# mLSTM gate preparation: two TensorE transposes replaced by VectorE-and-DMA turns, started one group earlier, with a head's masks added beside its keys

## The chip, the cores and the metric

The kernel runs on one core of a Trainium2 chip. The metric is device time in microseconds, from the first instruction to the last plus what lies around them. The core has a matrix engine (TensorE, "PE" in the profile, with its weight loads as "PEld"), VectorE (DVE), ScalarE (ACT), GpSimd (POOL) and SyncE (SP). SP computes nothing here; it issues most of the DMA transfers. Each engine takes its instructions strictly in the order of its own list and waits on semaphores for the others.

## The reference

One encoder block on 512 tokens of width 1024, all in float32:

```python
h = rms_norm(x, mix_norm_g[l])
proj = h @ w_in[l]      # mLSTM q,k,v,o,gates | attention q,k,v | memory q | merge gates
y_ml = mlstm_branch(...)             # 4 heads of 128, two directions
y_na = neighbourhood_attention(...)  # 8 heads on an 8 x 64 grid
y_xa = memory_cross_attention(...)   # 4 heads, 256 memory tokens
merged = g_ml * (y_ml @ w_br_ml[l]) + g_na * (y_na @ w_br_na[l]) + g_xa * (y_xa @ w_br_xa[l])
x = x + merged @ w_out[l]
x = x + conv_glu_ffn(rms_norm(x, ffn_norm_g[l]), ...)
return rms_norm(x, final_norm_g)
```

The change concerns the gates of the mLSTM. For each token, head and direction there is an input gate and a forget gate. The branch needs the running sum of the logarithm of the forget gate along the tokens of a chunk, and a running maximum that keeps the exponentials in range:

```python
log_f = jax.nn.log_sigmoid(f_pre)
a = jnp.cumsum(log_f, axis=-1)
D = a[..., :, None] - a[..., None, :] + log_i[..., None, :]
D = jnp.where(causal, D, -jnp.inf)
m_j = jnp.maximum(a + m_prev[..., None], jnp.max(D, axis=-1))
P = jnp.exp(D - m_j[..., None]) * qk
h = num / jnp.maximum(jnp.abs(den), jnp.exp(-m_j))[..., None]
```

The kernel computes the same with chunks of 128 tokens.

## The kernel before

**Matmuls.** Nearly every product is made in three passes (`mm3`, L334): both operands are split into a rounded high part and a low remainder, and high x high, high x low and low x high are added in PSUM. Activations are kept as high and low tiles (`XH`/`XL`, `NH`/`NL`). Weights come from DRAM in blocks of 1024 columns and more, three raw buffers ahead (`emit_raw`, L189, loads on SP). Each half of a block becomes a high piece by a ScalarE copy (L301) and a low piece by a VectorE subtraction (L302); there are four buffers for such pairs, so TensorE's progress frees them.

**The order of the stages.** First come the mLSTM queries and keys (feature-major), then three "token-major" groups (`TMW`, L598 to L620), in which the tokens lie on the partitions of the result: group 0 gives the gates `Gt` and half of the values, group 1 the other half and some attention values, group 2 the rest of the attention values. Inside a group the loop goes over weight blocks `h`, then over the four token tiles `t`, then over `k`. Then come four projections `xaq` (memory queries), four `o` (output gates), four `memk` and the four steps of `memv` (memory keys and values), four `naq` and four `nak` (attention queries and keys), and then three branches, each with merge gates and a projection. In a projection, 8 x 3 matmuls run on 512 tokens (256 for `memk`). The output projection and the feed-forward part follow.

**Steps between matmuls.** The mLSTM, the memory attention and the neighbourhood attention are Python generators (`ml_all`, `xa_all`, `na_all`), one behind the other in the list `gens`. `step(n)` (L1124) adds n to a quota and resumes the first generator once for each whole unit; the projections call it with 0.65 in the middle and 0.65 at the end (`mid`, `RB`), the memory blocks with 0.65 for each block, the merge gates with half a unit twice. Each `yield` ends a step. So the generators' small matmuls are placed in TensorE's list between the large ones. The first branch calls `drain` (L1204) before it reads the mLSTM result. The build's scheduler keeps this program order as a priority, but may place an instruction of VectorE, ScalarE, GpSimd or SP earlier on its engine where its inputs are ready.

**The gate preparation** (`ml_prep`, L637 to L730) has four steps:

1. the logarithm of the forget gate as 32 columns `lf`, by some twenty small VectorE operations;
2. `lfc` (tokens on partitions; log-forget at columns 0 and 32, input gate at 64 and 96) is turned into rows by four TensorE transposes with the identity (L670). ScalarE copies 36 of the rows (L672), and four scans on VectorE (L676, L677, L685, L686) make the running maximum `mr` and the running sum `cu`; a copy of `cu` goes to rows 64 to 100 of `mr`;
3. `rr = cu - mr`, written to DRAM as `rd`, and the chunk ends as a small diagonal tile `dg`;
4. the rows of head 0 are loaded broadcast to all partitions (`load_R`), head 0's turned keys are loaded (`turn_in`), four more TensorE transposes (L712) bring `mr` back to tokens on partitions, a product of ones with `dg` (L714) spreads the chunk ends, and the exponentials `em`, `bi`, `ex` follow.

**A turn** is what the kernel already uses for keys, heads and attention weights: `turn_out` (L166) transposes the 32 x 32 blocks of a 128 x 512 tile on VectorE (L169) and stores the result with four DMAs (L172) to a DRAM tile `td`; `turn_in` (L176) loads that tile (L178) with tokens and features exchanged.

**A head** is then `begin` (products of keys and queries L761, scaling of turned keys L764/L765), `middle` (states L801, L806, first diagonal tile L774/L778), `rest` (second diagonal tile), `last` (queries L788/L790, and the loads of the next head's rows and keys), and four `values_J` steps (L817 to L828). The rows `R` plus a causal mask are the masked rows `rm`; today `load_R` adds the masks (L742) as soon as the rows have landed. The last head is scaled (L837), turned, and written as high and low parts by `emit_y` (L841 to L847), which the first branch reads at its fourth k.

Of the kernel before, what the change touches and what calls it, by code (L numbers as in the profile page):

```python
# [11 lines left out]
F32 = mybir.dt.float32  # L12
# [5 lines left out]
P = 128  # L18
S = 512
D = 1024  # L20
KT = D // P
# [109 lines left out]
def hybrid_block(ctx, tc, xT, memT, wflat, vecs, gbias, nabias, out):  # L131
# [202 lines left out]
    def mm3(ps, lh, ll, rh, rl, start, stop):  # L334
        PE.matmul(ps, lh, rh, start=start, stop=False)  # L335
        PE.matmul(ps, lh, rl, start=False, stop=False)  # L336
        st["mm"] = PE.matmul(ps, ll, rh, start=False, stop=stop).ins  # L337
# [259 lines left out]
    xn_load()  # L597
    for c, n in enumerate(TMW):  # L598
        pss = [(mmps if c % 2 else atps)() for _ in range(NT)]
        g = 2 if n == 512 else 4  # L600
        for h in range(KT // g):
            ws = weights(("tm", c, h))
            if len(xs) < KT:
                xn_load()
            xn_part(2 * c + h if c < 2 else 6 + h)
            for t in range(NT):
                tsl = slice(t * P, (t + 1) * P)
                for k in range(g):
                    kk = g * h + k
                    mm3(pss[t][:, :n], XH[kk][:, tsl], XL[kk][:, tsl], ws[k][0], ws[k][1], kk == 0, kk == KT - 1)  # L610
        for t in range(NT):
            ps = pss[t]
            if c == 0:
                V.scalar_tensor_tensor(Gt[:, t, :], ps[:, :16], rc[:, t:t + 1], gb, op0=ALU.mult, op1=ALU.add)
                to_va(0, t, ps[:, 16:272])
            elif c == 1:
                to_va(1, t, ps[:, :256])
                to_nav(0, t, ps[:, 256:])
            else:
                to_nav(1, t, ps[:, :256])  # L620
# [16 lines left out]
    def ml_prep(load_R):  # L637
# [25 lines left out]
        lfc = cp.tile([P, NT, 100], F32, name="lfc")  # L663
# [4 lines left out]
        pl = atps()  # L668
        for t in range(NT):
            PE.transpose(pl[:100, t * P:(t + 1) * P], lfc[:, t, :], ident)  # L670
        lr = scr()
        A.activation(lr[:36], pl[:36, :], AF.Copy)  # L672

        mr = scr()
        G.memset(mr[:100], 0.0)
        V.tensor_tensor_scan(mr[0:4, :], lr[0:4, :], pl[64:68, :], NEG, op0=ALU.add, op1=ALU.max)  # L676
        V.tensor_tensor_scan(mr[32:36, ::-1], lr[32:36, ::-1], pl[96:100, ::-1], NEG, op0=ALU.add, op1=ALU.max)  # L677
# [4 lines left out]
        G.memset(onv[32:36, :, P - 1:P], 0.0)  # L682
        cu = tp.tile([P, 2 * M], F32, tag="nab", name=nm("cu"))
# [3 lines left out]
        A.activation(mr[64:100], cu[:36], AF.Copy)  # L687
        yield
# [22 lines left out]
        for t in range(NT):  # L711
            PE.transpose(pmv[:, t, :], mr[:100, t * P:(t + 1) * P], ident[:100, :100])  # L712
        pt = atps()
        PE.matmul(pt[:, :64], ones[:100], dg[:100].rearrange("p g t h -> p (g t h)"), start=True, stop=True)  # L714
        em = cp.tile([P, NT, 36], F32, name="em")
        A.activation(em, pmv[:, :, 0:36], AF.Exp, scale=-1.0)
# [15 lines left out]
    def ml_all():  # L732

        def load_R(h):
            rd = ml["rd"]
            R, rm = [], []
            for d in range(2):
                t = tp.tile([P, S], F32, tag="R", name=nm("R"), bufs=4)
                SY.dma_start(t, rd[d, h].partition_broadcast(P))
                R.append(t)  # L740
                t = tp.tile([P, S], F32, tag="R", name=nm("R"), bufs=4)
                V.tensor_tensor(t.rearrange("p (j c) -> p j c", j=4), R[d].rearrange("p (j c) -> p j c", j=4),  # L742
                                msk[d].unsqueeze(1).to_broadcast([P, 4, P]), op=ALU.add)
                rm.append(t)
            return R, rm
# [64 lines left out]
        def values_J(h, J, E, Q, C, H, ss):  # L810
# [11 lines left out]
            emv = em[:, J, :].rearrange("p (a b) -> p a b", b=4)  # L822
            V.tensor_tensor(den, den, emv[:, 0:9:8, h], op=ALU.max)
# [321 lines left out]
    gens.append(ml_all())  # L1145

# [432 lines left out]
```

## Time and profile before

| what | value |
|---|---|
| time, median of 3 runs | 858.54 us (858.33 to 858.70) |
| the profiled execution, its own time | 859.0 us |
| its span, first to last instruction | 857.2 us |
| granted TensorE clock, mean | 0.999 |
| instructions | 12212 |
| VectorE transposes (L169) | 40 |
| turn stores (L172) / turn loads (L178) | 160 / 40 |

The profile is one execution. The span is shorter than the execution's own time by 1.8 us that lie around it. A row of the timeline gives the start and the duration in us, the engine, the line of the kernel, the operation, the tile written and the tiles read, shapes, how many were merged into the row, and in brackets how long the engine had stood idle and who released it. A matmul's end is modelled and overlaps the next one's start. A row of the stages gives, for each engine, busy time and number of instructions, then the granted clock, the share of the DMA engines and GB/s.

### The profile page before, as it was taken

How to read it: one execution, taken by the hardware profiler on the slowest of the kernel's cores; microseconds unless marked ns; L12 is line 12 of the kernel's file. 1: busy time of each engine (PE TensorE's matmuls, PEld its weight loads, DVE VectorE, ACT ScalarE, POOL GpSimd, SP SyncE). 2: the span in 40 equal slices, each digit the busy share in tenths (PEclk: the TensorE clock that was granted, in tenths of full speed). 3: DMA queues.
4: the chain of work that ended last, by engine and by line, in shares of the span. 5: the costliest groups of instructions: out<-in, count | busy, mean ns of one | idle time of the engine just before them, and what ended most of it. 6: DMA issues, size and time to landing. Idle time of an engine off the chain costs nothing.

```text
span 857.2 us, 12212 instructions
## 1 busy us (share of the span) xinstructions
PE 849.3 (99%) x4059; PEld 714.0 (83%) x4059; DVE 606.5 (71%) x1219; ACT 458.5 (53%) x966; POOL 149.6 (17%) x235
## 2 busy tenths in 40 slices
PE   9999999999999999999999999999999999999996
PEld 7898988988888888888888888888888888888885
DVE  7699677875458658998586557767766677756773
ACT  7465556775446648888644445334444444533442
POOL 2000100000102830454000212111111111210211
PEclk9999999999999999999999999999999999999999
DMA  8236734543335846888623432444422223844842
GB/s 273 86 113 210 236 136 148 185 158 112 125 102 183 229 138 185 236 241 240 198 95 111 148 110 86 160 148 147 146 101 99 93 92 119 250 114 138 237 111 99
DMA packets 75103, 131.55 MB, mean 153 GB/s; under 512 B 10008, under 2 KB 35480, under 8 KB 75040
## 3 DMA queue, kind: packets, MB, share of 16 engines
q1 hardware_dynamic: 65088, 120.12, 43.2%
q0 software_dynamic: 9664, 10.51, 6.3%
q8 instruction: 32, 0.52, 0.3%
q14 instruction: 31, 0.25, 0.1%
q10 hardware_dynamic: 288, 0.14, 0.1%
HBM read 116.03 MB, written 14.70 MB: 153 GB/s over the span
## 4 chain that ended last, share of the span: by engine, by line
PE 96%; DMA 1%; DVE 1%; issue 1%; ACT 0%; SPq 0%; POOLq 0%; POOL 0%; ACTq 0%; DVEq 0%
PE mm L337 28%; PE mm L336 28%; PE mm L335 27%; PE at L335 3%; PE at L336 3%; PE at L337 3%; PE at L984 1%; PE at L817 1%; PE at L801 1%; PE at L819 1%; DMA U<-td 1%; DMA s<-xT 1%; PE at L951 0%; PE at L950 0%; PE at L761 0%
## 5 line engine op out<-in xcount | busy, mean ns | idle before, releaser
L335 PE MATMUL mm<-u,w 128*128 128x512 f32 (+1 forms) x912 | 353.7, 388 | 0.0
L337 PE MATMUL mm<-u,w 128*128 128x512 f32 (+1 forms) x912 | 352.1, 386 | 0.1
L336 PE MATMUL mm<-u,w 128*128 128x512 f32 (+1 forms) x912 | 352.0, 386 | 0.0
L301 ACT ACTIVATE w<-wr 128x512 fp32r<-128x512 f32 (+1 forms) x256 | 159.8, 627 | 134.1 <-PE mm L337 105.5
L302 DVE TENSOR_TENSOR w<-wr,w 128x512 fp32r<-128x512 f32 (+2 forms) x257 | 175.3, 686 | 69.7 <-ACT w L301 67.3
L337 PEld LDWEIGHTS mm<-u,w 128*128 128x128 f32 x912 | 171.3, 188 | 35.0 <-DVE w L302 0.7
L336 PEld LDWEIGHTS mm<-u,w 128*128 128x128 f32 x912 | 171.5, 188 | 33.8 <-DVE u L342 0.5
L335 PEld LDWEIGHTS mm<-u,w 128*128 128x128 f32 x912 | 171.5, 188 | 33.7 <-ACT w L301 0.3
L630 POOL DMA_DIRECT2D u<-nav_d x128 | 62.1, 500 | 101.8 <-PE at L984 52.4
L1299 POOL TENSOR_TENSOR s<-s,rb 128x512 f32<-128x512 f32 x21 | 35.7, 1701 | 180.2 <-DVE s L1297 172.5
L238 ACT ACTIVATE w<-u 128x512 fp32r<-128x512 f32 x48 | 30.2, 631 | 53.3 <-PE mm L337 41.0
L335 PE MATMUL mm<-w,u 128*128 128x512 f32 x144 | 56.2, 390 | 0.0
L336 PE MATMUL mm<-w,u 128*128 128x512 f32 x144 | 56.0, 389 | 0.0
L337 PE MATMUL mm<-w,u 128*128 128x512 f32 x144 | 56.0, 389 | 0.0
L238 DVE TENSOR_TENSOR w<-u,w 128x512 fp32r<-128x512 f32 x48 | 33.1, 691 | 29.3 <-ACT w L238 28.9
L337 PEld LDWEIGHTS mm<-w,u 128*128 128x128 f32 x144 | 27.0, 188 | 5.7
L335 PEld LDWEIGHTS mm<-w,u 128*128 128x128 f32 x144 | 27.0, 188 | 5.5
L336 PEld LDWEIGHTS mm<-w,u 128*128 128x128 f32 x144 | 27.0, 188 | 5.5
L341 ACT ACTIVATE u<-s 128x512 fp32r<-128x512 f32 x14 | 8.8, 632 | 36.1 <-DVE s L1307 36.1
L523 ACT ACTIVATE s<-pad,vec 128x512 f32<-128x512 f32 x30 | 24.4, 812 | 5.3 <-DVE pad L521 4.4
L524 DVE SCALAR_TENSOR_TENSOR s<-pad,vec,s 128x512 f32<-128x512 f32 x30 | 22.5, 749 | 4.0 <-ACT s L523 4.0
L1268 POOL TENSOR_TENSOR acc<-acc,s 128x512 f32<-128x512 f32 x7 | 9.0, 1290 | 92.9 <-ACT s L1267 92.9
(298 smaller groups left out, 1151.6 us busy)
## 6 DMA issues: line engine op xcount, KB each, us to landing
wr<-wflat SPq DMA_DIRECT2D x124, 512.0 KB, 3.4
u<-wflat SPq DMA_DIRECT2D x48, 256.0 KB, 4.8
td<-s SPq DMA_DIRECT2D x160, 64.0 KB, 2.0
U<-td SPq DMA_DIRECT2D x40, 256.0 KB, 3.5
s<-xT SPq DMA_DIRECT2D x24, 256.0 KB, 4.2
nab<-nabias SPq DMA_DIRECT2D x16, 256.0 KB, 3.8
u<-nav_d POOLq DMA_DIRECT2D x128, 32.0 KB, 3.4
u<-wflat POOLq DMA_DIRECT2D x16, 256.0 KB, 6.9
```

What stands on the lines that cost most here:

```text
L238: chain[eng] = getattr({"V": V, "A": A, "G": G}[eng], what)(*a, **k).ins
L301: A.activation(h[:, u:v], src, AF.Copy)
L302: V.tensor_tensor(l[:, u:v], src, h[:, u:v].bitcast(F32), op=ALU.subtract)
L335: PE.matmul(ps, lh, rh, start=start, stop=False)
L336: PE.matmul(ps, lh, rl, start=False, stop=False)
L337: st["mm"] = PE.matmul(ps, ll, rh, start=False, stop=stop).ins
L341: A.activation(h, src, AF.Copy, scale=scale)
L523: A.activation(t1, pad[:, 0:512], AF.Identity, scale=vcol(w, i), bias=vcol(b, i))
L524: V.scalar_tensor_tensor(t1, pad[:, 1:513], vcol(w, n + i), t1, op0=ALU.mult, op1=ALU.add)
L630: G.dma_start(vw[r * 32:(r + 1) * 32, i * 256:(i + 1) * 256], nav_v[hf, r, CW[b]:CW[b] + 32, hp * 256:(hp + 1) * 256])
L1268: G.tensor_tensor(acc2, acc2, sq, op=ALU.add)
L1299: chain["G"] = G.tensor_tensor(c, c, rb2, op=ALU.mult).ins
```

## The change

- The loop over the token-major groups moves down in the program, behind the creation of the `ml_all` generator. In group 2, after token tile 1 of each of the two weight blocks, it calls `step(1)`. So the first two steps of the generator stand inside that group.
- In `ml_prep`, `lfc` grows from 100 to 128 columns and is turned by `turn_out` and `turn_in` instead of TensorE. ScalarE copies two sets of 36 rows (`lr`, `gr`) out of the turned tile, one copy more, and the scans read `gr` where they read PSUM.
- `mr` is turned back by `turn_out` and `turn_in` too; `em` and `bi` read the turned tile `mt` instead of PSUM. `em` holds only the 2 x 4 x 4 columns that are used.
- The preparation has three more `yield`s: seven steps instead of four.
- `load_R` only loads. The masks are added by the new `masked`, which `begin` calls after `keys`.

The core of the diff:

```diff
+        lfc = cp.tile([P, NT, P], F32, name="lfc")
...
-        pl = atps()
-        for t in range(NT):
-            PE.transpose(pl[:100, t * P:(t + 1) * P], lfc[:, t, :], ident)
-        lr = scr()
-        A.activation(lr[:36], pl[:36, :], AF.Copy)
-
+        ld = turn_out(lfc)
         mr = scr()
-        G.memset(mr[:100], 0.0)
-        V.tensor_tensor_scan(mr[0:4, :], lr[0:4, :], pl[64:68, :], NEG, op0=ALU.add, op1=ALU.max)
...
+        G.memset(mr, 0.0)
...
+        yield
+        lt = turn_in(ld, "K", 1)
+        yield
+        lr, gr = scr(), scr()
+        for x, o in ((lr, 0), (gr, 64)):
+            A.activation(by4(x[:36]).rearrange("p s (i a) -> p s i a", i=4), lt[o:o + 36], AF.Copy)
+        V.tensor_tensor_scan(mr[0:4, :], lr[0:4, :], gr[0:4, :], NEG, op0=ALU.add, op1=ALU.max)
...
         A.activation(mr[64:100], cu[:36], AF.Copy)
+        md = turn_out(by4(mr))
         yield
...
         ml["R"] = load_R(0)
+        mt = turn_in(md, "K", 1).rearrange("p s i a -> p i s a")
         ml["K"] = turn_in(kd[0], "nab", 2)
-        pm = atps()
-        pmv = pm[:, :400].rearrange("p (t c) -> p t c", t=NT)
-        for t in range(NT):
-            PE.transpose(pmv[:, t, :], mr[:100, t * P:(t + 1) * P], ident[:100, :100])
+        yield
         pt = atps()
...
-        em = cp.tile([P, NT, 36], F32, name="em")
-        A.activation(em, pmv[:, :, 0:36], AF.Exp, scale=-1.0)
+        em = cp.tile([P, 2, NT, 4], F32, name="em")
+        A.activation(em, mt[:, 0:2, :, 0:4], AF.Exp, scale=-1.0)
...
-            V.tensor_tensor(bi[:, d], gv[:, :, d, 0, :], pmv[:, :, 64 + 32 * d:68 + 32 * d], op=ALU.subtract)
+            V.tensor_tensor(bi[:, d], gv[:, :, d, 0, :], mt[:, 2 + d, :, 0:4], op=ALU.subtract)
...
                 R.append(t)
+            return R
+
+        def masked(R):
+            rm = []
+            for d in range(2):
                 t = tp.tile([P, S], F32, tag="R", name=nm("R"), bufs=4)
...
         def begin(h):
             kt, C = own(h)
-            st_[h] = dict(kt=kt, C=C, kq=keys(h, kt), R=ml.pop("R"))
+            st_[h] = dict(kt=kt, C=C, kq=keys(h, kt), R=masked(ml.pop("R")))
...
     gens.append(ml_all())
+
+    xn_load()
+    for c, n in enumerate(TMW):
...
+                    mm3(pss[t][:, :n], XH[kk][:, tsl], XL[kk][:, tsl], ws[k][0], ws[k][1], kk == 0, kk == KT - 1)
+                    if c == 2 and t == 1 and k == 3:
+                        step(1)
```

More of the change, by code (lines that the diff above doesn't have):

```diff
@@ L662, in ml_prep @@
         yield
-        lfc = cp.tile([P, NT, 100], F32, name="lfc")
+        lfc = cp.tile([P, NT, P], F32, name="lfc")
         G.memset(lfc, 0.0)
@@ L682, in ml_prep @@
         G.memset(onv[32:36, :, P - 1:P], 0.0)
+        yield
[5 more added lines that the diff above has]
+        V.tensor_tensor_scan(mr[0:4, :], lr[0:4, :], gr[0:4, :], NEG, op0=ALU.add, op1=ALU.max)
+        V.tensor_tensor_scan(mr[32:36, ::-1], lr[32:36, ::-1], gr[32:36, ::-1], NEG, op0=ALU.add, op1=ALU.max)
         cu = tp.tile([P, 2 * M], F32, tag="nab", name=nm("cu"))
@@ L821, in values_J @@
             A.activation(den, pv[:, :, 128], AF.Abs)
-            emv = em[:, J, :].rearrange("p (a b) -> p a b", b=4)
-            V.tensor_tensor(den, den, emv[:, 0:9:8, h], op=ALU.max)
+            V.tensor_tensor(den, den, em[:, :, J, h], op=ALU.max)
             V.reciprocal(den, den)
@@ L1145, in hybrid_block @@
     gens.append(ml_all())
+    xn_load()
+    for c, n in enumerate(TMW):
+        pss = [(mmps if c % 2 else atps)() for _ in range(NT)]
+        g = 2 if n == 512 else 4
+        for h in range(KT // g):
+            ws = weights(("tm", c, h))
+            if len(xs) < KT:
+                xn_load()
+            xn_part(2 * c + h if c < 2 else 6 + h)
+            for t in range(NT):
+                tsl = slice(t * P, (t + 1) * P)
+                for k in range(g):
+                    kk = g * h + k
+                    mm3(pss[t][:, :n], XH[kk][:, tsl], XL[kk][:, tsl], ws[k][0], ws[k][1], kk == 0, kk == KT - 1)
+                    if c == 2 and t == 1 and k == 3:
+                        step(1)
+        for t in range(NT):
+            ps = pss[t]
+            if c == 0:
+                V.scalar_tensor_tensor(Gt[:, t, :], ps[:, :16], rc[:, t:t + 1], gb, op0=ALU.mult, op1=ALU.add)
+                to_va(0, t, ps[:, 16:272])
+            elif c == 1:
+                to_va(1, t, ps[:, :256])
+                to_nav(0, t, ps[:, 256:])
+            else:
+                to_nav(1, t, ps[:, :256])
     xq = unit()
```

27 lines of the change are left out of this document (1 added, 26 removed).

## The prediction

> **What bounds the kernel now.** I read the page's busy times and its chain of waits first, then busy time by stage, then the instructions of each engine in order of time around the gate preparation.
>
> ```profile
> span 857.2 us, 12212 instructions
> PE 849.3 (99%) x4059; PEld 714.0 (83%) x4059; DVE 606.5 (71%) x1219; ACT 458.5 (53%) x966; POOL 149.6 (17%) x235
> PE 96%; DMA 1%; DVE 1%; issue 1%; ACT 0%; SPq 0%; POOLq 0%; POOL 0%; ACTq 0%; DVEq 0%
> ```
>
> TensorE is busy for 99% of the span and is 96% of the chain that ends last, so a matmul taken away is time taken away, as long as nothing else becomes late. Busy matmuls overlap, so I go by the distance from one start to the next. The stages:
>
> ```profile
> core 0: us, PE busy (x) PEld busy (x) DVE busy (x) ACT busy (x) POOL busy (x), PEclk, DMA share, GB/s
> ...
> 95.50:119.30 23.80, 23.80 (x116) 19.83 (x115) 17.12 (x37) 12.26 (x25) 2.62 (x5) 1.00 0.48 152
> ...
> 146.40:175.50 29.10, 29.10 (x203) 26.98 (x202) 24.39 (x72) 21.84 (x67) 1.74 (x2) 1.00 0.52 172
> ...
> 284.00:302.00 18.00, 17.94 (x80) 14.38 (x78) 13.26 (x29) 12.47 (x31) 14.95 (x32) 1.00 0.77 208
> 302.00:430.00 128.00, 127.94 (x620) 107.82 (x621) 98.81 (x254) 93.82 (x224) 37.26 (x77) 1.00 0.71 210
> ```
>
> In the gate preparation (95.5 to 119.3) and the memory projections (146.4 to 175.5) TensorE shows no idle time at the full granted clock. Only the last two stages show any, 0.06 us each. VectorE is 72% busy in the first and 84% in the second: that is where extra work could turn into waiting.
>
> **The change, part by part.** *Eight TensorE transposes go.* They stand in TensorE's order of time like this:
>
> ```profile
> 106.22 0.40 PE L337 MATMUL mm<-u,w 128*128 128x512 f32 x1
> 106.45 0.60 PE L670 MATMUL at<-ident,lfc 128*100 128x128 f32 x4
> 106.81 0.48 PE L335 MATMUL mm<-u,w 128*128 128x512 f32 x1
> 107.12 0.40 PE L336 MATMUL mm<-u,w 128*128 128x512 f32 x1
> ...
> 114.39 0.51 PE L712 MATMUL at<-ident,s 100*128 100x100 f32 x4
> 114.80 0.41 PE L714 MATMUL at<-dg,ones 100*128 100x64 f32 x2
> ```
>
> A 128x512 matmul takes 0.23 us from start to start (106.22 to 106.45). The first four transposes hold TensorE from 106.45 to 106.81, 0.36 us, and the matmul behind them takes 0.31 instead of 0.23: 0.08 more. The other four take 114.80 - 114.39 = 0.41 us; the ones-by-dg product behind them stays and keeps its own switch. Together 0.36 + 0.08 + 0.41 = 0.85 us.
>
> *Two turns by VectorE and DMA come.* Each is one VectorE transpose of 128x512, four stores to DRAM and one load, the last five on SP's queue. The kernel already does this for keys and heads:
>
> ```profile
> L169 DVE STREAM_TRANSPOSE s<-H x4: 702/706/711, 172.3 to 225.2; 128x512 f32<-128x512 f32 x4
> ...
> L172 SPq DMA_DIRECT2D td<-s x160: 302/432/1684, 57.9 to 616.3; - x160
> DMA to landing us min/median/max: 1.6/2.0/5.1
> ...
> L178 SPq DMA_DIRECT2D U<-td x40: 319/334/384, 112.8 to 618.7; - x40
> DMA to landing us min/median/max: 2.6/3.5/6.7
> ```
>
> One turn takes 0.71 + 4 x 0.43 + 2.0 + 0.33 + 3.5 = 8.3 us from end to end, two take 16.6. SP's queue gets eight stores and two loads, 8 x 0.43 + 2 x 0.33 = 4.1 us of issue, and stands still while each turn's stores land; the weight loads queued behind it have three raw buffers, so they run about two blocks, 11 us, ahead of their use, which covers a landing of 5.1. VectorE gets 1.4 us. ScalarE gets two 36-row copies where it had one.
>
> *The start moves up.* Two steps of the generator now run inside the last token-major group, three more steps are put in, so all that follows the preparation comes one step later in program order.
>
> ```profile
> L666 POOL COPY lfc<-lf x2: 655/692/730, 72.8 to 73.4; 128x16 f32<-128x16 f32 x2
> ...
> 107.15 0.58 ACT L672 ACTIVATE s<-at 36x512 f32<-36x512 f32 x1
> ...
> 107.81 1.22 DVE L676 TENSOR_TENSOR_SCAN s<-s,at 4x512 f32<-4x512 f32 x1 [1.91 <-issue]
> ...
> 112.74 0.69 DVE L302 TENSOR_TENSOR w<-wr,w 128x512 fp32r<-128x512 f32 x1
> ...
> 124.00 0.69 DVE L742 TENSOR_TENSOR R<-R,msk 128x512 f32<-128x512 f32 x1 [3.81 <-DMA R<-rd]
> ...
> 127.59 0.69 DVE L302 TENSOR_TENSOR w<-wr,w 128x512 fp32r<-128x512 f32 x1
> ...
> 127.90 0.50 PE L801 MATMUL at<-u,u 128*128 128x129 f32 x3
> ```
>
> The gate tile is complete at 73.4 + 0.7 = 74.1 today and then lies until TensorE reaches the transposes at 106.45. The second step's place is two projections of 24 x 0.23 = 5.5 us and half a 5.8 us block before that, at 92.6. A turn begun there is back at 100.9, two copies of 0.58 end it at 102, and the four scans (107.81 to 112.74, 4.9 us) end near 107 instead of 112.7. The second turn follows a copy of 0.6 and is back near 116. Head 0's state matmuls, which need its result, end with the three at 127.90 and now stand a 5.5 us projection later, near 132.5. With some 2 us (an estimate) for the small products and the scaling of keys between, the two trips are hidden by about 14 us; two slowest landings (5.1 and 6.7 for 2.0 and 3.5, 6.3 us more per turn, 12.6 for both) would use that cover up but not exceed it. I cost the turns at nothing on the path. POOL's fills and copies are the same ones, earlier; the stores of the attention values that share its queue are read long after.
>
> The older rows go the other way from a rule of the Trainium skill: the page "VectorE: DVE Perf Modes", section "Rules for kernel authors", sends a 128x128 transpose to TensorE where PSUM will do as its target. By the rule nothing is to be won here, and the kernel stays at 858.5 or loses; the rows say that the 0.85 us lie on the engine that sets the end, while the turn's 8.3 us lie beside it. What the rule would make of the time is the third rival.
>
> *The waits that the change adds.* ScalarE's copies wait for the turned gates, VectorE's scans for ScalarE, and weight pieces queue behind both. How much waiting is free is shown by today's mask: VectorE stood 3.81 us before it at 124.00 and the next weight piece was done only at 127.59 + 0.69 = 128.28. Its user:
>
> ```profile
> 128.92 0.39 PE L335 MATMUL mm<-u,w 128*128 128x512 f32 x1
> ```
>
> The low piece is read by the third matmul of the triple, two starts later at 129.38, so 1.1 us were left. A wait of 3.8 + 1.1 = 4.9 us is thus covered. The nearest row for the new wait is the scans' 1.91 us; the far one is 1.91 + 6.3 = 8.2, if both landings of a turn are the slowest seen. I take the near one, since the medians are close to the fast ends: 0, with 8.2 - 4.9 = 3.3 us as the far end.
>
> *The masks move* from the load of a head's rows to its keys, a step later. The eight additions stay; the wait of 3.81 goes, off the path, since rows are loaded a step before. What VectorE waits for next there is the turned keys. Gain on the path 0. Their cost if cover is missing belongs to the second rival.
>
> *The end of the branch comes a step later too.* Head 3's rows are written directly in front of the branch's first projection:
>
> ```profile
> 219.50 0.39 PE L817 MATMUL at<-u,E 128*128 128x129 f32 x2
> ...
> 234.34 0.69 DVE L847 TENSOR_TENSOR u<-s,u 128x512 fp32r<-128x512 f32 x1
> ...
> 241.53 0.39 PE L335 MATMUL mm<-u,w 128*128 128x512 f32 x1
> ```
>
> The last values product starts at 219.50, the low half of head 3 is done at 235.03, and its first reader, the matmul after the one at 241.53, starts at 241.76: 6.7 us to spare. The values move one 5.5 us projection towards it, so 1.2 us remain. I cost this at 0; if the load lands in 6.7 instead of 3.5, 3.2 - 1.2 = 2.0 us come out. It cannot be a gain.
>
> **The sum.** 0.85 off, 0 added. The profiled execution took 859.0 us (857.2 span and 1.8 around it) and would take 858.15. It stood 0.46 above the median 858.54, and from the median I predict 857.7.
>
> **The rivals.** *Given back in short waits.* What is saved is returned in small pieces, at head 3's 1.2 us or behind a late gate tile within its cover: from 858.5 (the change does nothing for the time) to 857.7 + 2.0 = 859.7. For it: the margin there shrinks from 6.7 to 1.2. Against: the sequence from the values on moves by a whole projection, so it keeps its place among the weight pieces.
>
> *Slower: VectorE in the memory key projections.* These blocks are half as long, and one place has nothing to spare today:
>
> ```profile
> 138.29 0.69 DVE L742 TENSOR_TENSOR R<-R,msk 128x512 f32<-128x512 f32 x1 [0.64 <-DMA R<-rd]
> ...
> 143.96 0.73 DVE L778 TENSOR_TENSOR E<-E,at 128x256 f32<-128x256 f32 x2
> ...
> 152.98 1.29 DVE L302 TENSOR_TENSOR w<-wr,w 128x512 fp32r<-128x512 f32 x2
> ...
> 153.52 0.28 PE L336 MATMUL mm<-u,w 128*128 128x256 f32 x1
> 153.73 0.38 PE L337 MATMUL mm<-u,w 128*128 128x256 f32 x1
> ```
>
> The matmul at 153.73 starts 0.21 us after its neighbour where 0.12 is usual: it waits for the first of the two pieces begun at 152.98. Head 1's masks (the second at 138.29) and the four products of its diagonal tiles (two in 0.73 us at 143.96) are done before this stage today. In the new order the masks come with its keys, at the end of the stage before, and the products behind them. If all 2 x 0.69 + 4 x 0.37 = 2.9 us push pieces, the result is 857.7 + 2.9 = 860.6. It ends up slower by over 0.2% from 2.6 us. Against it: VectorE has 29.10 - 24.39 = 4.7 us free in the stage, some work leaves it at the other end, and the stage before, with the 3.81 us wait gone, hands over with more in store.
>
> *Slower: a turn shows.* The price is the far end above, 857.7 + 3.3 = 861.0; it decides from a wait of 4.9 + 2.6 = 7.5 us. For it: ScalarE and VectorE take their lists in order, so one late tile holds all weight pieces. Against: both landings have to be the slowest of 160 and 40. This is what the skill's transpose rule, named above, would lead to.
>
> *Faster than the sum.* Besides the 0.85 the waits of the attention stages could happen to go: 0.12 by the stages' rows, and in the chain one values group that took 1.05 where its neighbours take 0.47:
>
> ```profile
> 377.34 0.47 PE at L984 x4
> ...
> 383.82 1.05 PE at L984 x4
> ```
>
> That is 0.58 more, in all 858.54 - 0.85 - 0.12 - 0.58 = 857.0. Nothing in the change touches those stages, and even so it stays within 0.2%.
>
> **How the numbers follow.** 0.2% (1.7 us) is about what a measurement of this kernel can tell from no change. Forecast 857.7: 0.50, with 857.4 to 858.2 for itself. Given back: 0.20. Memory projections: 0.15. A turn shows: 0.10. Faster than the sum: 0.05, and I give these 5 in 100 to "faster by over 0.2%" in case TensorE's order holds more slack than its rows show. So faster 0.05, within 0.2% 0.70, slower 0.25. The range goes from 857.0 to 861.0, the prices of the outermost cases; half of the rarest two and some of the memory case lie outside, under 2 in 10.
>
> **What would show it.** Right: 4051 matmuls on PE, none from the gate tile by the identity; td stores x168, U loads x42; scans that start before 105; no wait of TensorE near 106 to 119; head 3's low half done ahead of its reader by about 1 us; the same end of chain. Wrong: matmul starts over 0.3 us apart between 95 and 175 or at the first branch projection, weight pieces begun right after a wait for U or td, VectorE near full from 146 to 160. A difference of more than 1 us behind 300 would mean that the build reordered stages that the change does not touch, and my sum would be of the wrong place.

## The result, and the profile after

The changed kernel takes 859.94 us (median of 20 executions, 858.11 to 862.21); the kernel before, run beside it, 858.83 (20 executions, 857.95 to 860.1). The ratio is 1.0014, with a 95% interval of 1.0008 to 1.002: slower by 1.2 us, small against the 0.2% of the prediction but outside the interval, where 0.85 us less was forecast. The forecast of 857.7 was wrong; the range of 857.0 to 861.0 holds the time.

A part of the loss lies in no trace. What an execution takes beyond its span, from the first instruction to the last, is 1.72 to 1.84 us in every execution of the kernel before whose span is on record beside it, and 2.06 to 2.17 us in all of the changed kernel: about 0.34 of the 1.2 us. The prediction carried the 1.8 over unchanged. The term is a property of each kernel: 1.8 us in the kernel before with any of the edits below, with the third early step, and in the kernels without the norm; 2.1 in the changed kernel with most other edits; 2.4 to 2.5 by the median in two of them (the masks at the load, and the third early step together with the earlier norm). No view shows what fills it, so its cause stays open.

The profiled execution of the changed kernel happens to be its fastest, 858.11 us, 0.89 under the profiled execution of the kernel before. So this trace has to be read for what is *near* to costing time, and a second trace of the same kernel for what costs it. From the page of the changed kernel (span; busy time, share of the span and number of instructions; shares of the chain of waits; DMA issues with size and median us to landing):

```profile
span 856.0 us, 12212 instructions
...
PE 847.9 (99%) x4051; PEld 713.4 (83%) x4051; DVE 606.4 (71%) x1221; ACT 460.0 (54%) x967; POOL 150.1 (18%) x235
...
PE 97%; ACT 1%; DMA 1%; DVE 1%; issue 0%; SPq 0%; POOL 0%; POOLq 0%; ACTq 0%; DVEq 0%
...
td<-s SPq DMA_DIRECT2D x168, 64.0 KB, 1.9
U<-td SPq DMA_DIRECT2D x42, 256.0 KB, 3.6
```

The eight transposes are gone (4059 matmuls to 4051), two turns have come (160 stores and 40 loads to 168 and 42), the end is TensorE's as before.

The gate preparation in the timeline of the changed kernel (start, duration, engine, line, operation; the bracket tells idle time before it and who ended it), and below it the stage's row (busy us of PE, PEld, DVE, ACT, POOL, then the granted clock, DMA share and GB/s):

```profile
89.27 0.70 DVE L169 STREAM_TRANSPOSE s<-lfc 128x512 f32<-128x512 f32 x1
...
105.70 1.21 DVE L662 TENSOR_TENSOR_SCAN cu<-on,s 4x512 f32<-4x512 f32 x1
...
109.17 1.19 DVE L663 TENSOR_TENSOR_SCAN cu<-on,s 4x512 f32<-4x512 f32 x1
...
111.61 0.71 DVE L169 STREAM_TRANSPOSE s<-s 128x512 f32<-128x512 f32 x1
...
123.26 0.26 DVE L700 TENSOR_TENSOR bi<-Gt,U 128x16 f32<-128x16 f32 x2 [1.91 <-DMA U<-td]
...
128.63 0.67 DVE L746 TENSOR_SCALAR u<-U,ex 128x128 f32<-128x128 f32 x3
...
131.48 1.50 PE L782 MATMUL at<-u,u 128*128 128x129 f32 x12
```

```profile
95.50:119.30 23.80, 23.80 (x109) 19.73 (x108) 16.34 (x31) 12.62 (x24) 2.10 (x4) 1.00 0.58 183
```

TensorE has no idle time in that stage. But the second turn took 123.26 - 111.61 = 11.65 us from its transpose to its first user, and head 0's states start at 131.48, 2.2 us after the last of the scaled keys that they read (128.63 + 0.67): this cover is much thinner than forecast.

The loss inside the span is elsewhere. The view of waits has one entry for TensorE that the kernel before does not have (us in total, times, longest):

```profile
PE at L782 <- DVE H L806: 0.5, 1, 0.5
```

L782 are the states of head 1, and what they wait for is the last VectorE product of head 0's first values (L806). The two share no data. What they share is the `at` pool with its four tiles in PSUM, called banks below: the second half of the states wants the one in which those values still lie (the view names the wait; that it is for the bank follows from the program). The timeline of the changed kernel around it:

```profile
136.04 0.69 DVE L723 TENSOR_TENSOR R<-R,msk 128x512 f32<-128x512 f32 x1 [1.69 <-DMA R<-rd]
...
142.24 0.39 PE L800 MATMUL at<-u,E 128*128 128x129 f32 x2
...
142.78 0.28 DVE L436 CUSTOM_DVE_ANT_0 s<-at,ident 128x128 f32<-128x128 f32 x1
...
143.49 0.73 POOL L439 TENSOR_TENSOR rc_m<-y,nhalf 128x2 f32<-128x2 f32 x1 [29.29 <-DVE y L436]
...
144.26 0.20 ACT L441 ACTIVATE y<-rc_m 128x2 fp32r<-128x2 f32 x1 [2.20 <-POOL rc_m L439]
...
146.14 0.16 ACT L802 ACTIVATE y<-at 128x2 f32<-128x2 f32 x1
...
147.12 0.83 PE L782 MATMUL at<-u,u 128*128 128x129 f32 x6
...
148.01 0.34 DVE L806 SCALAR_TENSOR_TENSOR H<-at,y,H 128x128 f32<-128x128 f32 x1
...
148.50 0.91 PE L782 MATMUL at<-u,u 128*128 128x129 f32 x6 [0.55 <-DVE H L806]
```

The last product of the values starts at 142.24, and ScalarE could read them at about 142.6. But in front of that read (L802) stands L441, a step of a piece of work that the prediction never names: the *norm of the memory tokens*. It runs in the last `o` projection (function `rstd_cols`, called from L1163): a TensorE sum, two reductions on VectorE (L436), a power on GpSimd (L439), small copies on ScalarE (L441, L443, L444) and four products on VectorE. ScalarE stands still for 2.20 us until GpSimd is done, and head 0's values behind it. The same rows of the kernel before:

```profile
142.73 0.16 ACT L821 ACTIVATE y<-at 128x2 f32<-128x2 f32 x1
...
144.60 0.35 DVE L826 SCALAR_TENSOR_TENSOR H<-at,y,H 128x128 f32<-128x128 f32 x1
...
145.17 1.51 PE L801 MATMUL at<-u,u 128*128 128x129 f32 x12
...
146.55 0.28 DVE L436 CUSTOM_DVE_ANT_0 s<-at,ident 128x128 f32<-128x128 f32 x1
...
148.03 0.20 ACT L441 ACTIVATE y<-rc_m 128x2 fp32r<-128x2 f32 x1 [2.12 <-POOL rc_m L439]
```

There the values come first (142.73, 144.60), the norm behind them (146.55, 148.03), and the twelve state matmuls run in one piece. In the program the norm is written into a fixed projection and did not move; the values come one step later and have changed places with it.

### The profile page after: what moved, and what is told of

It reads as the page before. It is cut to its first block, busy times and chain, and to the rows that moved or that the text cites. A ratio compares the mean times of both kernels' runs of the same rounds, so it can differ in the third digit from the quotient of the medians.

```text
span 856.0 us, 12212 instructions
## 1 busy us (share of the span) xinstructions
PE 847.9 (99%) x4051; PEld 713.4 (83%) x4051; DVE 606.4 (71%) x1221; ACT 460.0 (54%) x967; POOL 150.1 (18%) x235
## 4 chain that ended last, share of the span: by engine, by line
PE 97%; ACT 1%; DMA 1%; DVE 1%; issue 0%; SPq 0%; POOL 0%; POOLq 0%; ACTq 0%; DVEq 0%
PE mm L337 28%; PE mm L335 28%; PE mm L336 28%; PE at L335 3%; PE at L336 3%; PE at L337 3%; PE at L964 1%; PE at L798 1%; DMA s<-xT 1%; PE at L782 1%; PE at L800 1%; PE at L930 0%; PE at L931 0%; PE at L742 0%; DVE w L302 0%
## 5 line engine op out<-in xcount | busy, mean ns | idle before, releaser
L238 POOL DMA_DIRECT2D u<-wflat x16 | 14.4, 965 | 61.6 <-DVE u L238 34.9
```

The costliest lines, as they stand in the source:

```text
L238: chain[eng] = getattr({"V": V, "A": A, "G": G}[eng], what)(*a, **k).ins
```

## The experiments

The theories, in the order in which they came up: G, the turned gates hold up weight pieces or land late; S, the shift by one step lets head 1's states ask for a PSUM bank too early; M, the masks in the memory stage (the prediction's second rival); J, short waits from late landings all over, owed to no one place; then N, the norm's place, as above; and R, some further cost of the shift. Each set of kernels was run beside the kernel before, on another chip than the set ahead of it, so kernels of different sets are compared by their ratios to it; a ratio of 0.001 is 0.86 us.

**The same kernel once more.**

> The changed kernel once more, for a second profiled execution. Theory G (the gates' turn): VectorE's four scans now stand in one block ahead of both weight pieces of the fourth memory-query projection, and the block starts when the turned gates and the memory tiles have landed; in the profile at hand the first piece is done 0.9 us before the first matmul that uses that buffer. An execution in which a landing comes later makes TensorE wait there, so the slow executions (up to 862.2) should show a wait of 1 to 4 us at the fourth memory-query projection (near 112 us) and nothing new elsewhere. Theory S (the step shift): the slow executions show the wait at the memory key projections (near 147 us), where TensorE waits 0.55 us for a PSUM bank in the profile at hand, grown to 1 to 4 us. Time by both: 858 to 862, median near 859.9.

859.93 us, ratio 1.0018 (1.0007 to 1.0028). This execution took 858.89 us, 0.78 more than the first profiled one, and the wait has grown:

```profile
136.90 0.69 DVE L723 TENSOR_TENSOR R<-R,msk 128x512 f32<-128x512 f32 x1 [1.17 <-DMA R<-rd]
...
143.64 0.28 DVE L436 CUSTOM_DVE_ANT_0 s<-at,ident 128x128 f32<-128x128 f32 x1
...
148.87 0.35 DVE L806 SCALAR_TENSOR_TENSOR H<-at,y,H 128x128 f32<-128x128 f32 x1
...
149.36 0.91 PE L782 MATMUL at<-u,u 128*128 128x129 f32 x6 [1.34 <-DVE H L806]
```

Head 1's mask, which waits for its rows from DRAM, is 0.86 us later than in the first trace; so are the norm's reduction (143.64 against 142.78) and the values' product (148.87 against 148.01). TensorE's wait grows by 0.79, because the states had come 0.07 later themselves. How late those rows land differs from execution to execution, which fits the wide spread of this kernel. No trace of one of its longest executions was kept.

**The masks alone, in the kernel before.**

```diff
-            st_[h] = dict(kt=kt, C=C, kq=keys(h, kt), R=ml.pop("R"))
+            st_[h] = dict(kt=kt, C=C, kq=keys(h, kt), R=masked(ml.pop("R")))
```

> The kernel before with nothing but the masks moved from a head's load to its keys; TensorE's transposes, the four steps and their places stay. Theory G: same as before within 0.05% (858.8), narrow spread of 1 to 2 us. Theory S: the same, since no step moves. Rival M (the masks on VectorE in the memory key projections): slower than before by 0.5 to 1.5 us, with waits of TensorE between 146 and 160.

860.11 us, ratio 1.0013 (1.0005 to 1.0022): this part costs time by itself, against what G and S expected. Not where theory M has it, though. Its timeline:

```profile
137.57 0.68 DVE L747 TENSOR_TENSOR R<-R,msk 128x512 f32<-128x512 f32 x1
...
138.18 0.99 DVE L811 SCALAR_TENSOR_TENSOR u<-u,ex,at 128x129 f32<-128x129 f32 x3
...
139.31 0.46 PE L824 MATMUL at<-u,E 128*128 128x129 f32 x2 [1.02 <-DVE u L811]
```

In the old step order the mask of head 1 stands on VectorE in front of head 0's state products, and head 0's first values wait 1.02 us for them. (A second wait of this execution, 0.5 us, lies in the memory attention.)

**The changed kernel with the masks at the load again** (the edit above, taken back).

> The changed kernel with the masks added at the load again; turns, early start and step shift stay. Theory G: no better than the changed kernel (859.5 to 860.5, wide spread), perhaps worse where VectorE waits for a head's rows. Theory S: the same. Rival M: back to 858.8 or below, since the masks leave the memory stage.

861.46 us, ratio 1.0028 (1.0018 to 1.0039): worse than the kernel before, and not back to it as M expected. Some 0.65 us of it lie outside the span. In the new order a mask at the load is a wait on VectorE ahead of the norm:

```profile
143.48 0.69 DVE L718 TENSOR_TENSOR R<-R,msk 128x512 f32<-128x512 f32 x1 [2.84 <-DMA R<-rd]
...
145.63 0.28 DVE L436 CUSTOM_DVE_ANT_0 s<-at,ident 128x128 f32<-128x128 f32 x1
...
150.86 0.35 DVE L801 SCALAR_TENSOR_TENSOR H<-at,y,H 128x128 f32<-128x128 f32 x1
...
151.35 1.02 PE L777 MATMUL at<-u,u 128*128 128x129 f32 x6 [3.17 <-DVE H L801]
```

With the first two traces this makes a series: reduction at 142.78, 143.64, 145.63; values' product at 148.01, 148.87, 150.86; TensorE's wait 0.55, 1.34, 3.17. Reduction and product move by exactly the same 0.86 and 2.85, and the wait by 0.79 and 2.62, which is that less the 0.07 and 0.23 by which the states came later. In these three traces a delay of the norm reached TensorE one for one.

The longest of these waits has a second price. Behind it, from 152.0 to 155.4, the granted clock is 0.50 and the matmuls of half length start 0.21 us apart, against 0.12 before and after: 15 of them, about 1.5 us more. Behind the waits of 0.55 and 1.34 us it stays at 1.00.

**One of the three new steps taken out,** so that head 0 begins at its old place:

```diff
-        yield
         lt = turn_in(ld, "K", 1)
```

> The changed kernel with one yield of the preparation taken out (the loads of head 0 in the same step as the chunk ends), so that head 0 begins after the fourth memory-query projection as before, not a step later. Theory S: the wait for the PSUM bank at the memory keys goes and the time falls below before, to 857.8 to 858.3 with a spread under 2 us. Theory G: the scans still stand ahead of the pieces, so it stays at 859.5 to 860.5 with the wide spread, less 0.5 at the most.

859.31 us, ratio 1.0007 (0.9997 to 1.0016), with a spread of 857.48 to 862.45, neither S's time and narrow spread nor clearly G's. The profiled execution was the slowest. The bank wait is gone in it, but the loads came late, of the memory's tokens, head 0's rows and the second turn (the row of `bi`):

```profile
123.35 0.69 DVE L722 TENSOR_TENSOR R<-R,msk 128x512 f32<-128x512 f32 x1 [5.47 <-DMA R<-rd]
...
126.83 0.26 DVE L699 TENSOR_TENSOR bi<-Gt,U 128x16 f32<-128x16 f32 x2 [0.66 <-DMA U<-td]
...
128.84 1.70 PE L781 MATMUL at<-u,u 128*128 128x129 f32 x12 [1.23 <-issue]
```

Head 0's states then start 1.23 us late (the view names no releaser; the keys that they read were being scaled just then, from 128.36 on). TensorE waits for other things too: 0.5 us for the chunk ends at 115.33, 1.2 in the memory attention and 0.7 for a weight piece. With the old step and the late start of the turns, a turn can show: the step of shift that costs time at 148 is also what covers the turn at 128. The run does not separate the two.

**The norm one projection earlier,** in the changed kernel:

```diff
-        if f == 2:
+        if f == 1:
             mp = rstd_parts(macc, M)
-        ps = proj(("o", f), NH, NL, at=mid({4: lambda: norm.append(rstd_cols(mp, M, "m"))} if f == 3 else {}))
+        ps = proj(("o", f), NH, NL, at=mid({4: lambda: norm.append(rstd_cols(mp, M, "m"))} if f == 2 else {}))
```

> The changed kernel, with the norm of the memory (the sum over POOL and ScalarE's square root) one projection earlier than the memory keys, so that ScalarE no longer stands still for it in front of head 0's values. Theory S (the shift by one step puts head 1's states behind a PSUM bank that head 0's values free late, through the chain mask, VectorE's part of the norm, POOL, ScalarE): the wait of TensorE at 147 to 148.5 is gone or under 0.3 us, the median falls by about 1 to 1.5 us, to 858.3 to 859.0, and the slow end of the runs comes down from 862.5 to about 861. If the bank is not the cause (theory J: short waits all over, from late landings, none of them owed to one place): same as the changed kernel, 859.9, with the spread of 858.3 to 862.5.

860.34 us, ratio 1.0018 (1.0009 to 1.0026): a miss. Where the bank wait stood, 0.17 us is left, but ScalarE's stand for GpSimd now holds up weight pieces, for which TensorE waits 0.82 at 145.94.

**A third early step,** so that the three new steps and the early ones cancel and all that follows stands in its old step:

```diff
-                    if c == 2 and t == 1 and k == 3:
+                    if (c == 2 and t == 1 and k == 3) or (c == 1 and h == 3 and t == 1 and k == 1):
```

> The changed kernel with a third early step, in the second token-major group, so that the three steps put in and the three early ones cancel and all that follows the preparation stands in the old step. Theory S: no bank is asked for in the first memory key projection, as before the change; no wait at 147 to 148.5; median 857.9 to 858.6, about the forecast sum. Theory J: 859.3 to 860, spread as in the changed kernel. The rival of late turns is also touched: they have one projection less of cover behind and one more ahead, so a wait near 123 to 128 would speak for it.

858.41 us, ratio 0.9998 (0.9989 to 1.0007), spread 857.45 to 859.35. The turns, the masks and the rest of the change are all in it; only the shift is gone, and with it 1.4 us by the ratios (0.3 of them outside the span), the bank wait and the upper end of the spread. The view of waits shows none of TensorE's but the one at the start of the kernel (1.2 us, which all these kernels have).

**The norm one projection earlier in the kernel before, and with the third early step.**

> Control: the kernel before with the norm of the memory one projection earlier. Theory S: there is no bank wait there to remove, so 858.8 within 0.4. If this alone is faster by 1 us, a gain of the first run of this set is not owed to what the change did.

> The changed kernel with both: a third early step and the norm one projection earlier. Theory S: with the old step the norm's place no longer matters, so the same as with the third early step alone within 0.4; if anything it is the fastest, 857.7 to 858.4. Theory J: 859.3 to 860.

860.36 us, ratio 1.0021 (1.0012 to 1.003), and 860.13, ratio 1.0018 (1.0009 to 1.0027). Both expectations failed, and they turned the theory. (Of the second's 1.5 us, 0.7 lie around the span; in the span the bank wait is back with 0.91 us.) The kernel before, in its old step order, with the norm moved ahead of head 0's first values:

```profile
142.03 0.28 DVE L436 CUSTOM_DVE_ANT_0 s<-at,ident 128x128 f32<-128x128 f32 x1
...
147.27 0.34 DVE L826 SCALAR_TENSOR_TENSOR H<-at,y,H 128x128 f32<-128x128 f32 x1
...
147.75 0.91 PE L801 MATMUL at<-u,u 128*128 128x129 f32 x6 [1.30 <-DVE H L826]
```

This is the wait of the changed kernel, made without the change. So it is not the shift that asks for the bank too early (S): it is the norm in front of the values (N).

**The norm half a stage later,** in the changed kernel and in the kernel before: its sum at `f == 3`, its square root in the second `memk` projection, its row product in the third.

> The changed kernel with the norm of the memory half a stage later: its sum in the last output-gate projection's place, its square root in the second memory key projection instead of the fourth output-gate projection, so that it stands behind head 0's first values on VectorE, POOL and ScalarE, as it does in the kernel before. Theory N (what costs the time is that the shift by one step puts this norm in front of those values, which hold the PSUM bank that head 1's states need): no TensorE wait at 147 to 149, those values' last VectorE product 3 to 4 us earlier than 148.0, median 858.0 to 858.8, slow end under 860.5. If the shift costs by something else (late landings over the whole stage, theory J): 859.6 to 860.2 as the changed kernel. If the norm now runs late for the keys of the memory, a wait of TensorE near 152 to 156 says so.

> Control: the kernel before with the same edit. There the norm stands behind the values already, so theory N expects nothing of it: 858.4 to 859.3. If it is faster by about as much as the first run of this set against the changed kernel, the norm's later place is a gain of its own, and says nothing of the shift.

859.16 us, ratio 1.0009 (1.0001 to 1.0018), and 859.1, ratio 1.001 (1.0001 to 1.0019). The bank wait is gone in the first. But this place has its own price of about 0.5 us: in both, the norm's row product (L455) is late. The profiled execution of the first, 861.21, also waited 1.5 us before 289.72 for a turned tile of the memory attention, in a stage that no edit touches; the granted clock then is 0.50 from 291 to 294. The first kernel lies between what N and J expected, 858.0 to 858.8 and 859.6 to 860.2, so this does not decide.

**The third early step again, and the transposes doubled** (each of the eight done twice into the same place, in the kernel before).

> The changed kernel with the third early step once more, for its interval: 858.0 to 858.8 by theory N, at 0.9990 to 1.0000 of the time before; 859.3 or more if the first result was luck.

> The kernel before with each of the eight TensorE transposes done twice into the same place: it prices what the change takes off TensorE. By the prediction's rows, 0.36 + 0.41 = 0.77 us more (the 0.08 of the switch comes only once): 859.3 to 859.8. If it is within 0.3 us of the kernel before, the transposes lie beside a wait and nothing could be won by taking them away; if it is over 1.5 us, they are dearer than their rows.

858.13 us, ratio 0.9997 (0.9988 to 1.0006): the first result holds. Doubled transposes: 859.11, ratio 1.0008 (0.9999 to 1.0017), that is 0.5 to 0.7 us more than before, where 0.77 was expected; the median lies just under the expected range. The trace prices them directly:

```profile
106.61 1.03 PE L671 MATMUL at<-ident,lfc 128*100 128x128 f32 x8
107.40 0.48 PE L335 MATMUL mm<-u,w 128*128 128x512 f32 x1
...
114.99 0.85 PE L714 MATMUL at<-ident,s 100*128 100x100 f32 x8
115.68 0.36 PE L716 MATMUL at<-dg,ones 100*128 100x64 f32 x2
```

The two groups hold TensorE for 0.79 and 0.69 us, where the single ones held it for 0.36 and 0.41: 0.71 more.

**The exchange alone:** in the changed kernel the norm's square root is written directly behind the step with head 0's first values.

```diff
-        ps = proj(("o", f), NH, NL, at=mid({4: lambda: norm.append(rstd_cols(mp, M, "m"))} if f == 3 else {}))
+        ps = proj(("o", f), NH, NL, at=mid())
...
+    norm.append(rstd_cols(mp, M, "m"))
     mrc = norm[2][0]
```

> The changed kernel with one neighbourly exchange: the memory norm's square root is written directly behind the step that computes head 0's first values, instead of inside the projection ahead of it. Nothing else moves by more than some 3 us. Theory N: those values' last VectorE product runs 3 to 4 us earlier than the 148.0 of the changed kernel, head 1's states find their bank free, and the median is 858.0 to 858.8. Theory R (the shift costs by something else as well): 859.2 or more, with no wait at 147 to 149.

859.04 us, ratio 1.0004 (0.9995 to 1.0013): 0.9 us of the loss is back. The median lies between the two expectations. The bank wait is gone, and the view of waits names what is late next, the row product that follows the norm:

```profile
PE at L455 <- DVE y L803: 1.1, 1, 1.1
```

**Without the norm,** in the changed kernel, in the kernel before and with the third early step.

> The changed kernel with the memory norm's sum, reduction and power left out (a constant column stands for them; ScalarE's and VectorE's small steps behind them stay), so that nothing of the norm is waited for. Theory N: 858.0 to 858.8 less the sum's matmul, and faster than the kernel before without that norm, by 0.4 to 0.9. Theory R: slower than the kernel before without that norm by 0.4 or more.

> Control: the kernel before with the memory norm's sum, reduction and power left out, as in the run ahead of it. Theory N: 858.3 to 858.8, since its norm made nobody wait; theory R the same.

> The changed kernel with the third early step and without that norm. Theory N: within 0.4 of the changed kernel without the norm, since the shift costs only by the norm's place. Theory R: faster than it by 1 us or more, which is what the shift costs elsewhere.

857.74 us, ratio 0.9989 (0.9981 to 0.9998); 859.16, ratio 1.0 (0.9991 to 1.0009); 858.05, ratio 0.9996 (0.9987 to 1.0005). The control came out above its forecast, in two clusters of executions, around 858 and from 858.9 up. Where nobody waits for the norm, the change is a gain: 0.9989 against 1.0, or 0.9 us by the ratios. The two intervals just touch; the means of the eleven executions of each, 857.78 and 858.89, differ by 1.1 us, give or take 0.6. And the kernel with the shift is no slower than the one without it (857.74 and 858.05), where R asked for 1 us or more: R has failed.

**The exchange, and the row product one projection later,** with nothing left out:

```diff
-        ps_m.append(proj(("memk", f), MH, ML, M, at={4: lambda: norm.append(rstd_row(norm[2][1], M, "m"))} if f == 1 else {}))
-        for i in range(2 if f == 1 else 1):
-            to_mk(f - 1 + i if f == 1 else f, ps_m.pop(0))
+        ps_m.append(proj(("memk", f), MH, ML, M, at={4: lambda: norm.append(rstd_row(norm[2][1], M, "m"))} if f == 2 else {}))
+        for i in range(0 if f == 1 else 3 if f == 2 else 1):
+            to_mk(f - 2 + i if f == 2 else f, ps_m.pop(0))
```

> The exchange of the norm and head 0's first values once more, and with it the norm's row product one memory key projection later, so that the wait of 1.19 us for it, which the exchange alone brought, has cover. Nothing is left out. Theory N: neither a wait for the PSUM bank at 147 to 149 nor one for the row product at 150.6; 857.6 to 858.2, 0.9985 to 0.9997 of the kernel before, as the changed kernel without the norm (857.74). If the row product now runs late at its new place, 858.6 to 859.2 with a wait near 154.

858.3 us, ratio 0.9996 (0.9987 to 1.0005), spread 857.26 to 859.32: 1.5 us less than the changed kernel by the ratios, the median 0.1 above the expected range. Both waits are gone. Its timeline:

```profile
137.90 0.69 DVE L723 TENSOR_TENSOR R<-R,msk 128x512 f32<-128x512 f32 x1 [2.02 <-DMA R<-rd]
...
144.82 0.15 ACT L802 ACTIVATE y<-at 128x2 f32<-128x2 f32 x1
...
146.70 0.35 DVE L806 SCALAR_TENSOR_TENSOR H<-at,y,H 128x128 f32<-128x128 f32 x1
...
147.39 1.50 PE L782 MATMUL at<-u,u 128*128 128x129 f32 x12
...
149.63 0.20 ACT L441 ACTIVATE y<-rc_m 128x2 fp32r<-128x2 f32 x1 [1.63 <-POOL rc_m L439]
```

The rows of head 1 came even later than in the second trace of the changed kernel (137.90 against 136.90), and the states still run in one piece. The stage's rows, of the changed kernel and then of this one:

```profile
140.00:160.00 20.00, 19.45 (x156) 18.89 (x155) 17.19 (x49) 13.47 (x41) 0.73 (x1) 1.00 0.51 173
```

```profile
140.00:160.00 20.00, 20.00 (x161) 19.47 (x160) 17.77 (x54) 15.06 (x47) 1.11 (x1) 1.00 0.64 197
```

In time it is level with the kernel before within what can be measured, so no version that keeps the norm beats the kernel before by more than the interval. In span it is ahead: 856.2 against 856.8 us by the medians, 0.7 less by the means, give or take 0.5. The 2.13 us that lie around its span, against 1.77, take half of that back.

## Why the prediction was wrong

**The step that failed** is "three more steps are put in, so all that follows the preparation comes one step later in program order". I costed the delay at nothing after looking at two things: whether the delayed work was still ready for its readers (head 0's states, head 3's end), and whether the new waits were covered. I did not ask what the delayed work *passes* that does not move with it. The memory's norm is tied to a projection, the head's steps to the generator, and one step of delay put the norm's chain over three engines in front of head 0's values. What the runs showed in place of nothing is 1.4 to 1.5 us, from the changed kernel to the same with the third early step (1.0014 against 0.9998 and 0.9997). Some 1.2 of them lie in the span, and the exchange with the later row product, which leaves the shift in, brings all of that back. The other 0.3 lie around the span, a second term that the prediction left as it was (1.8, and 2.1 in the changed kernel).

**The sum.** Eight transposes at 0.85 us: right in kind, and no run contradicts the size. Doubling them holds TensorE for 0.71 us more in the trace and costs 0.5 to 0.7 in time, where 0.77 was expected; without the norm the change gains about 1. The Trainium skill, page "VectorE: DVE Perf Modes", section "Rules for kernel authors", sends a 128x128 transpose to TensorE where PSUM will do as its target; here that place costs the bounding engine these tenths, and the loss that came with leaving it was not the turn's. The whole kernels that keep the norm and avoid its place (858.41, 858.13, 858.3) show 0.3 to 0.5 us of the saving in the medians, with intervals of some 0.8 us to either side that hold both 0.85 and 0. For the last of them the rest is found: its span is 0.6 to 0.7 us shorter, and 0.36 is lost around it. For the third early step the rest was not settled.

**The turns** are hidden where forecast: no TensorE wait from 95.5 to 119.3. Their size was wrong. The scans start at 105.70, where a start before 105 was named as a sign of being right, and end at 110.4 and not near 107. The second turn takes 11.65 us and not 8.3, and from its first user to the last scaled key it is 129.30 - 123.26 = 6.0 us, where an estimate of 2 stood that no row was given for. So the cover at head 0's states is 2.2 us and not about 14; that it was enough owes something to luck. Nothing was paid for that in the two traces of the changed kernel; the run with one new step fewer shows that it can be.

**The masks.** "Gain on the path 0" did not hold in the old order, and in the new one it is not shown. In the old order they cost 0.0013 (1.1 us) with the keys; in the new order they come out 0.0010 dearer at the load than with the keys (1.0028 against 1.0018, beside each other), a difference that the intervals do not separate and of which a third lies around the span. What they cost depends on which instruction stands behind them on VectorE.

**Head 3's end** had 1.2 us to spare by the forecast and no wait. None came: in the first trace its low half is done at 239.44 and read at 241.36, 1.9 us later.

**The rivals.** "Given back in short waits" has the size (858.5 to 859.7, against 858.54 x 1.0014 = 859.7) and one of its traits, a wait that depends on how late a load lands, but neither of its places. "VectorE in the memory key projections" names the right stage with the wrong mechanism: TensorE waits there for a bank and not for weight pieces. "A turn shows" did not happen in the traces of the changed kernel, and "Faster than the sum" did not happen at all. The spread was not foreseen: the kernel before reaches from 857.95 to 860.1, the changed one from 858.11 to 862.21.

## What to carry to other kernels

When work is moved in an in-order list, write down what it overtakes or falls behind on every engine, above all short chains that cross several engines (here VectorE, GpSimd, ScalarE): the chain's stand-still is free or not depending only on what queues behind it. A wait between two pieces of work that share no data can be a buffer; look for who still holds it and what stands in front of that one's last read. And when an experiment moves a suspect, run the same move in the kernel before: that control overturned the first theory here, because the move had a price of its own. Look, too, at what an execution takes outside its span before a difference of tenths is looked for inside it.

## What the runs showed that was not expected

- A TensorE wait can come from a chain over four engines that begins at a DMA landing some 12 us earlier (136.90 to 148.87 in the second trace): rows 0.86 us later made the norm's reduction and the values' last product 0.86 us later, one for one by way of VectorE, GpSimd, ScalarE and VectorE to TensorE.
- A wait of TensorE can cost more than its length. Behind waits of 3.17 us (masks at the load) and 1.5 us (norm half a stage later) the granted clock was 0.50 for about 3 us; behind waits of 1.34, 1.30 and 1.23 us no row shows it below 1.00. Of the changed kernel's 32 executions the seven with a mean clock of 0.997 or less all took over 861.3 us, and only two of the others did. That fits the same cause for the upper end of its spread, but no trace of such an execution was kept, and executions of the kernel before reach 0.997 with no such loss.
- The rows of a head, written by GpSimd's queue and read back broadcast by SP's, land 3.1 to 4.6 us after their issue in the trace of the kernel before and 3.1 to 5.3 in those of the changed kernel. The mask of head 1 that waits for them started at 136.04, 136.90 and 137.90 in three traces, the last that of the exchange with the later row product.
- The fastest execution of a kernel can hide its loss: the profiled one was 0.9 us faster than that of the kernel before, the median 1.1 slower.
